# Sparse attention scores: low part of the keys on 64 partitions, multiplied with the high part of the queries alone

## The chip, the cores and the metric

The kernel runs on one core of a Trainium2 chip. The metric is the device time of one execution in microseconds; lower is better. The profile is one execution recorded by the hardware profiler, and its times count from the start of its span.

## What is computed

The reference is a decoder trunk with two layers over 512 tokens of width 1024. Each layer is a half-step feed-forward part, a token mixer, cross-attention into 256 memory tokens, and another feed-forward part. The mixer of layer 0 is causal pooling; that of layer 1 is native sparse attention with 16 query heads in 4 groups, one key head and one value head per group, and a head width of 64. The part that matters here are the scores of its selected-block and sliding-window branches:

```python
q = q.reshape(B, S, G, R, dh).transpose(0, 2, 3, 1, 4) * dh ** -0.5
...
sc = jnp.einsum('bgrqd,bgqkd->bgrqk', qb, ksel)
...
sc = jnp.einsum('bgrqd,bgkd->bgrqk', qb, kwin)
```

With 512 tokens both branches see every earlier token, so the kernel computes both as causal attention over the same range, each with keys and values of its own, and a third branch over 31 compressed blocks per key head.

## The kernel before, in words

Products run on TensorE in fp32r, a rounded form of fp32. To keep the precision the kernel splits an operand into a high part (the rounded value) and a low part (what is left of it): `split` (L413) lets ScalarE (ACT) copy the source into the high part (L415) and VectorE (DVE) subtract that from the source into the low part (L416). A dense product then takes three matmuls, high x high, high x low and low x high (`mm3`, L401, with L403 to L405). The weights are streamed from DRAM by SP and split in the same way, by ACT (L334) and by DVE or GpSimd (POOL) (L374).

Heads are only 64 wide, so a score product fills half of the 128 rows of the array. The kernel before uses the other half for the low part of the queries. `qproj` (L1259) makes, for each query head, one tile `qst` of 128 partitions: the high part in one half, the low part in the other. For even heads the high part is in partitions 0 to 63, for odd heads in 64 to 127. `kproj` (L1246) makes, for each key head, two tiles `kst`, one with the high and one with the low part of the keys of both branches, and it writes each part twice, to partitions 0 to 63 and to 64 to 127, so that both halves of `qst` meet the same keys. `kproj` therefore issues four ACT copies and four DVE subtractions per key head, each of 64 x 512:

```python
for br in range(2):
    src = kf[br * 64:(br + 1) * 64]
    for r0 in (0, 64):
        self.split([a[r0:r0 + 64, br, :] for a in t], src)
```

`mm4` (L407) then needs two matmuls for a score: `qst` with the high keys (L410) and `qst` with the low keys (L411). It contains all four products of the parts.

`softmax` (L1331) calls `mm4` for each of 64 units (4 groups, 4 query heads, 4 blocks of 128 queries). For the first two blocks one call makes both branches, for the last two there is one call per branch. This gives 96 calls, with 256, 512, 384 or 512 columns each. `cmp_scores` (L1289) multiplies the whole `qst` with compressed keys `kcz`, which stand in both halves of the partitions too.

The order of the work is written out by hand. `NSA_START` is a string that says how the steps of the compressed keys' hidden layer (`hidden`, `cmp_k_hidden`, `cmp_k`), of the first key head and of the first query heads follow each other; `cmp_k_hidden` splits a transposed tile into `hidT`. Then the units run in a loop with softmax, transposes into `pT` (L1369), and products with the values (`values`, L1374 to L1382) three units later. The table `FILL` says how many steps of the next key and query heads' projections go between the units, and `CMP` when the compressed branch's steps run (`cmp_transposed`, L1323, writes `pTc`). Within one engine the instructions run in the order in which they were placed when the program was built; across engines they wait on semaphores.

Of the kernel before, what the change touches and what calls it, by code (L numbers as in the profile page):

```python
# [6 lines left out]
F32 = mybir.dt.float32  # L7
# [388 lines left out]
class Kernel:  # L396
# [9 lines left out]

    def mm4(self, ps, a, b, start, stop, **kw):  # L407

        mm = self.nc.tensor.matmul
        mm(ps, a, b[0], start=start, stop=False, **kw)  # L410
        mm(ps, a, b[1], start=False, stop=stop, **kw)  # L411

    def split(self, hl, src):  # L413

# [680 lines left out]
    def nsa(self, gnext):  # L1095
        nc, small, att = self.nc, self.small, self.att
# [149 lines left out]
        def kproj(g):  # L1246
            ps = self.bank("psk")
            yield from self.dense_steps(ps, ("nsa_w_k", g * P), xg)
            kf = self.tmp("kf")
            nc.vector.tensor_mul(kf, ps, self.rbc)  # L1250
            t = [self.b4("kst") for _ in range(2)]
            for br in range(2):
                src = kf[br * 64:(br + 1) * 64]
                for r0 in (0, 64):
                    self.split([a[r0:r0 + 64, br, :] for a in t], src)
            kst[g] = t
            yield

        def qproj(g, cs=(0, 1)):  # L1259
            for c in cs:  # L1260
                ps = self.bank("psq")
                yield from self.dense_steps(ps, (W_NSA, g * 256 + c * P), xg)
                for b in range(2):
                    t = self.b2("qst")
                    self.split((t[b * 64:(b + 1) * 64], t[(1 - b) * 64:(2 - b) * 64]), ps[b * 64:(b + 1) * 64])
                    qst[g, 2 * c + b] = t
                yield

# [9 lines left out]
        def fill(g):  # L1278
            if g < NG - 1:
                yield from kproj(g + 1)  # L1280
                yield from qproj(g + 1)
            else:
                yield from self.mem_k(1, 0)
            if g > 0:
                yield from wo(2 * g - 2, 2 * g, False)
            if g == NG - 1:
                yield from self.mem_k(1, 1)
# [157 lines left out]
        kc2 = blocks(1)  # L1445
        vproj(1, {})
        parts = {"A": hidden(0, kc), "K": kproj(0), "Q": qproj(0, (0,)), "B": hidden(1, kc2), "R": qproj(0, (1,))}
        for c in NSA_START:
            if c in parts:
# [113 lines left out]
```

## Time and profile before

| what | value |
|---|---|
| three executions | 2070.29, 2070.99, 2071.24 us (median 2070.99) |
| the profiled execution's own time | 2072.0 us |
| its span, first to last instruction | 2070.3 us |
| mean granted TensorE clock | 0.996 |
| TensorE (PE) busy | 2051.1 us, 99% of the span |
| VectorE (DVE) busy | 1549.8 us, 75% |
| ScalarE (ACT) busy | 1128.5 us, 55% |
| GpSimd (POOL) busy | 184.4 us, 9% |

PE stands for matmuls and PEld for loads of their weights, which overlap the matmuls. A matmul's record is longer than its step to the next one, because the ends overlap; so the step from start to start tells what a matmul costs in a dense stretch. A shape such as 128*128 128x512 gives the rows and columns of the weights and the rows and columns of what streams past them.

### The profile page before, as it was taken

To read this page: it belongs to the slowest core of one execution; us is meant where nothing else is said; L and a number is where in the kernel's file an instruction comes from. 1 tells how busy PE (TensorE), PEld (TensorE's weight loads), DVE (VectorE), ACT (ScalarE), POOL (GpSimd) and SP (SyncE) were. 2 spreads that over 40 slices of the span, in tenths; PEclk is the share of its full clock that TensorE was granted. 3 is DMA by queue.
4 is the path that set the end of the run, shared out by engine and by line. 5 is a ranking of instruction groups with operands and counts; after the bars stand their busy time and mean duration, and the time that the engine had idled before them with its cause. 6 is when DMAs were issued, how large, how long until landed. Compare 5 with 4: busy or idle time off the path is not lost.

```text
span 2070.3 us, 33527 instructions
## 1 busy us (share of the span) xinstructions
PE 2051.1 (99%) x12373; PEld 1832.8 (89%) x12373; DVE 1549.8 (75%) x2828; ACT 1128.5 (55%) x2275; POOL 184.4 (9%) x261
## 2 busy tenths in 40 slices
PE   9999999999999999999999999999999999999998
PEld 7899998988889999888999988888998888899997
DVE  8777976965877777688777757788976458777774
ACT  6445555554545445554545545787775545454453
POOL 0000000000000000000000023444552100000000
PEclk9999999999999999999999999999999999999999
DMA  5333323532333332334333234311224223423322
GB/s 163 118 107 115 120 67 103 154 101 61 96 124 97 110 108 65 102 92 132 94 106 112 62 94 122 92 32 42 62 62 137 84 72 94 136 94 107 97 67 77
DMA packets 112501, 200.92 MB, mean 97 GB/s; under 512 B 12624, under 2 KB 20176, under 8 KB 112336
## 3 DMA queue, kind: packets, MB, share of 16 engines
q1 hardware_dynamic: 111920, 198.46, 31.2%
q8 instruction: 97, 1.59, 0.3%
q14 instruction: 68, 0.56, 0.1%
q10 hardware_dynamic: 416, 0.32, 0.1%
HBM read 196.63 MB, written 2.10 MB: 96 GB/s over the span
## 4 chain that ended last, share of the span: by engine, by line
PE 95%; DVE 2%; DMA 1%; ACT 1%; issue 0%; SPq 0%; POOL 0%; DVEq 0%; ACTq 0%
PE psr L405 10%; PE psr L403 10%; PE psr L404 10%; PE psy L404 10%; PE psy L403 10%; PE psy L405 10%; PE pso L1381 2%; PE psq L403 2%; PE psq L404 2%; PE psq L405 2%; PE psg L405 1%; PE psg L403 1%; PE psg L404 1%; PE psf L403 1%; PE psf L405 1%; PE psf L404 1%
## 5 line engine op out<-in xcount | busy, mean ns | idle before, releaser
L334 ACT CAST whl<-wraw 128x512 fp32r<-128x512 f32 (+3 forms) x688 | 416.3, 609 | 345.3 <-PE psy L405 99.5
L374 DVE TENSOR_TENSOR whl<-wraw,whl 128x512 fp32r<-128x512 f32 (+1 forms) x634 | 434.7, 688 | 221.2 <-ACT whl L334 206.5
L403 PE MATMUL psr<-rhs,whl 128*128 128x256 f32 x1764 | 500.3, 284 | 2.2 <-ACT whl L334 2.1
L405 PE MATMUL psr<-rhs,whl 128*128 128x256 f32 x1764 | 499.4, 284 | 0.8 <-DVE whl L374 0.8
L404 PE MATMUL psr<-rhs,whl 128*128 128x256 f32 x1764 | 499.8, 283 | 0.0
L403 PEld LDWEIGHTS psr<-rhs,whl 128*128 128x128 f32 x1764 | 338.9, 192 | 6.6 <-ACT whl L334 3.8
L404 PEld LDWEIGHTS psr<-rhs,whl 128*128 128x128 f32 x1764 | 339.0, 192 | 2.8
L405 PEld LDWEIGHTS psr<-rhs,whl 128*128 128x128 f32 x1764 | 338.7, 192 | 1.6 <-DVE whl L374 1.4
L404 PE MATMUL psy<-hT,whl 128*128 128x512 f32 (+1 forms) x710 | 276.3, 389 | 0.0
L403 PE MATMUL psy<-hT,whl 128*128 128x512 f32 (+1 forms) x710 | 275.9, 389 | 0.0
L405 PE MATMUL psy<-hT,whl 128*128 128x512 f32 (+1 forms) x710 | 275.0, 387 | 0.0
L334 ACT CAST whl<-wsum 128x512 fp32r<-128x512 f32 x252 | 156.7, 622 | 196.2 <-PE psy L405 150.5
L374 DVE TENSOR_TENSOR whl<-wsum,whl 128x512 fp32r<-128x512 f32 x252 | 173.3, 689 | 59.1 <-ACT whl L334 57.2
L405 PEld LDWEIGHTS psy<-hT,whl 128*128 128x128 f32 x710 | 133.4, 188 | 27.8
L404 PEld LDWEIGHTS psy<-hT,whl 128*128 128x128 f32 x710 | 133.6, 188 | 25.6 <-DVE hT L416 1.2
L403 PEld LDWEIGHTS psy<-hT,whl 128*128 128x128 f32 x710 | 133.6, 188 | 25.3
L374 POOL TENSOR_TENSOR whl<-wraw,whl 128x512 fp32r<-128x512 f32 (+2 forms) x54 | 68.2, 1265 | 817.8 <-ACT whl L334 803.7
L730 DVE SCALAR_TENSOR_TENSOR x<-psy,x 128x512 f32<-128x512 f32 x120 | 82.6, 688 | 41.5 <-PE psy L405 40.8
L1362 POOL TENSOR_SCALAR pr<-pr,smn,gates 128x128 f32<-128x128 f32 (+3 forms) x128 | 85.8, 683 | 103.9 <-DVE smn L1360 98.3
L1353 ACT ACTIVATE pr<-pr,mxn 128x128 f32<-128x128 f32 (+3 forms) x128 | 71.3, 559 | 14.3 <-DVE mxn L1349 13.1
L403 PE MATMUL psq<-xg,whl 128*128 128x512 f32 x192 | 76.0, 396 | 0.0
L404 PE MATMUL psq<-xg,whl 128*128 128x512 f32 x192 | 75.6, 394 | 0.0
(305 smaller groups left out, 3933.8 us busy)
## 6 DMA issues: line engine op xcount, KB each, us to landing
wraw<-wts SPq DMA_DIRECT2D x708, 256.0 KB, 2.7
wraw<-wts SPq DMA_DIRECT2D x21, 128.0 KB, 2.5
wraw<-wts SPq DMA_DIRECT2D x14, 192.0 KB, 2.6
x<-xT SPq DMA_DIRECT2D x8, 256.0 KB, 5.4
mraw<-memT SPq DMA_DIRECT2D x4, 512.0 KB, 3.0
out<-y SPq DMA_DIRECT2D x7, 256.0 KB, 2.4
wraw<-wts SPq DMA_DIRECT2D x8, 152.0 KB, 2.1
out<-y ACTq DMA_DIRECT2D x1, 256.0 KB, 3.1
```

The costliest lines, as they stand in the source:

```text
L334: nc.scalar.copy(self.hl[q][:, 0, :w], src[:, :w])
L374: eng.tensor_sub(hl[:, 1, :w], src[:, :w], hl[:, 0, :w].bitcast(F32))
L403: mm(ps, a[0], b[0], start=start, stop=False, **kw)
L404: mm(ps, a[0], b[1], start=False, stop=False, **kw)
L405: mm(ps, a[1], b[0], start=False, stop=stop, **kw)
L730: nc.vector.scalar_tensor_tensor(self.x[m], ps, 0.5, self.x[m], op0=ALU.mult, op1=ALU.add)
L1353: nc.scalar.activation(pr[br][:, :nk], pr[br][:, :nk], AF.Exp, bias=mx[:, br:br + 1], scale=-1.0, accum_out=sums[:, br:br + 1])
L1362: nc.gpsimd.tensor_scalar(pr[br][:, :nk], pr[br][:, :nk], sums[:, br:br + 1], gt[:, i, h * 3 + 1 + br:h * 3 + 2 + br], op0=ALU.mult, op1=A ...
L1381: nc.tensor.matmul(ps[:, c0:c0 + 256], v[br][j][:, g, :], pT[br][:, hl, j, :], start=False, stop=br == 1 and j == 2 * i2 + 1 and hl == 1)
```

## The change

The low part of the keys is written to partitions 0 to 63 only, and the queries' high part always stands in partitions 0 to 63, the low part in 64 to 127. The second matmul of `mm4` uses these 64 partitions alone: it multiplies the high part of the queries with the low part of the keys. The product of both low parts is left out. The high keys are still written to both halves.

```diff
     def mm4(self, ps, a, b, start, stop, **kw):
...
         mm = self.nc.tensor.matmul
         mm(ps, a, b[0], start=start, stop=False, **kw)
-        mm(ps, a, b[1], start=False, stop=stop, **kw)
+        mm(ps, a[:64], b[1][:64], start=False, stop=stop, **kw)
...
             for br in range(2):
                 src = kf[br * 64:(br + 1) * 64]
                 for r0 in (0, 64):
-                    self.split([a[r0:r0 + 64, br, :] for a in t], src)
+                    nc.scalar.copy(t[0][r0:r0 + 64, br, :], src)
+                nc.vector.tensor_sub(t[1][:64, br, :], src, t[0][:64, br, :].bitcast(F32))
             kst[g] = t
...
                 for b in range(2):
                     t = self.b2("qst")
-                    self.split((t[b * 64:(b + 1) * 64], t[(1 - b) * 64:(2 - b) * 64]), ps[b * 64:(b + 1) * 64])
+                    self.split((t[:64], t[64:]), ps[b * 64:(b + 1) * 64])
                     qst[g, 2 * c + b] = t
```

## Rows read from the trace of the kernel before

**Rows 1.** The page, engines: busy us, share of the span, instructions.
```profile
PE   2051.1 (99%) x12373; PEld 1832.8 (89%) x12373; DVE 1549.8 (75%) x2828; ACT 1128.5 (55%) x2275; POOL 184.4 (9%) x261
```

**Rows 2.** The page, chain that ended last, by engine.
```profile
PE 95%; DVE 2%; DMA 1%; ACT 1%; issue 0%; SPq 0%; POOL 0%; DVEq 0%; ACTq 0%
```

**Rows 3.** By stretch: us; busy PE, PEld, DVE, ACT, POOL; granted clock, DMA share, GB/s.
```profile
1290.70:1294.30 3.60, 1.12 (x6) 0.53 (x4) 3.48 (x6) 3.43 (x7) 0.22 (x1) 1.00 0.37 112
1294.30:1301.10 6.80, 6.37 (x24) 5.79 (x25) 4.22 (x12) 2.67 (x8) 2.29 (x2) 0.50 0.30 99
...
1299.00:1545.00 246.00, 242.85 (x1526) 215.88 (x1525) 209.95 (x590) 190.30 (x514) 116.73 (x154) 1.00 0.20 59
```

**Rows 4.** What PE waited for, 1290 to 1545 us: total, times, longest.
```profile
PE psk L403 <- ACT hidT L415: 2.2, 1, 2.2
PE psc L1295 <- DVE qst L416: 1.6, 2, 1.3
PE psk L404 <- DVE hidT L416: 0.7, 1, 0.7
PE pso L1381 <- DVE pT L416: 0.6, 1, 0.6
...
PE pso L1377 <- DVE pTc L416: 0.4, 1, 0.4
```

**Rows 5.** Instructions on kst and qst: ns min/median/max, first and last start.
```profile
L415 ACT CAST kst<-kf x16: 615/618/624, 1290.3 to 1444.8; 64x512 fp32r<-64x512 f32 x16
L416 DVE TENSOR_TENSOR kst<-kf,kst x16: 675/690/1157, 1291.4 to 1445.9; 64x512 fp32r<-64x512 f32 x16
...
L416 DVE TENSOR_TENSOR qst<-psq,qst x16: 683/688/694, 1295.2 to 1468.0; 64x512 fp32r<-64x512 f32 x16
```

**Rows 6.** Timelines of DVE and ACT at key head 0: start, us.
```profile
1291.39 2.83 DVE L416 TENSOR_TENSOR kst<-kf,kst 64x512 fp32r<-64x512 f32 x4
1294.26 0.43 DVE L416 TENSOR_TENSOR hidT<-pst,hidT 128x256 fp32r<-128x256 f32 x1
...
1292.86 0.37 ACT L415 CAST hidT<-pst 128x256 fp32r<-128x256 f32 x1
```

**Rows 7.** Timelines of DVE and PE behind key head 1: start, us, [idle before].
```profile
1334.39 0.68 DVE L416 TENSOR_TENSOR pTc<-pst,pTc 128x512 fp32r<-128x512 f32 x1
...
1334.37 0.28 PE L1377 MATMUL pso<-pTc,vz 128*128 128x256 f32 x1
...
1335.12 0.39 PE L1377 MATMUL pso<-pTc,vz 128*128 128x256 f32 x1 [0.36 <-DVE pTc L416]
```

**Rows 8.** Timeline of DVE at key head 3.
```profile
1442.68 1.40 DVE L416 TENSOR_TENSOR kst<-kf,kst 64x512 fp32r<-64x512 f32 x2
...
1444.82 2.20 DVE L416 TENSOR_TENSOR kst<-kf,kst 64x512 fp32r<-64x512 f32 x2
1447.05 0.76 DVE L416 TENSOR_TENSOR pT<-pst,pT 128x256 fp32r<-128x256 f32 x2
```

**Rows 9.** Second score products: ns min/median/max, first and last start, shapes.
```profile
L411 PE MATMUL pss<-kst,qst x96: 278/388/415, 1300.0 to 1543.5; 128*128 128x512 f32 x48, 128*128 128x384 f32 x32, 128*128 128x256 f32 x16
```

**Rows 10.** Timeline of PE, dense products and transposes.
```profile
1369.78 0.82 PE L1369 MATMUL pst<-identf,pr 128*128 128x128 f32 x6
...
1370.61 0.34 PE L411 MATMUL pss<-kst,qst 128*128 128x384 f32 x1
1370.79 0.34 PE L410 MATMUL pss<-kst,qst 128*128 128x384 f32 x1
...
1371.14 0.39 PE L403 MATMUL psk<-xg,whl 128*128 128x512 f32 x1
1371.37 0.40 PE L404 MATMUL psk<-xg,whl 128*128 128x512 f32 x1
...
1372.07 0.60 PE L1326 MATMUL pst<-identf,pc 128*128 128x128 f32 x4
...
1372.74 0.40 PE L405 MATMUL psk<-xg,whl 128*128 128x512 f32 x1
```

## The prediction, made before the changed kernel was run

> **What bounds the kernel now.** I read the engine shares first, then the chain, then a stretch. PE is busy 99% of the span and DVE 75% [rows 1], and 95% of the chain that ended last is PE's [rows 2]: time comes off only where PE stands still or where its own work gets shorter, and whatever is added to PE's work counts in full. The change touches only the sparse attention of layer 1. From 1299 to 1545 us, where the scores are made, PE is busy 242.85 of 246 us [rows 3], so there is hardly a gap in which a dearer product could hide. The list of PE's waits shows what is left of gaps there [rows 4]: 2.2 us on an ACT copy of hidT, 1.6 us on qst, and three waits on DVE (hidT 0.7, pT 0.6, pTc 0.4). The last three are the ones that this change could reach, as the timelines will show.
>
> **Subtractions taken away.** For each of four key heads the kernel makes four ACT copies and four DVE subtractions of kst; 16 subtractions stand in the trace, 0.69 us at the median [rows 5]. The change keeps the copies and drops two subtractions per head, 8 x 0.69 = 5.5 us of DVE work. Most of it lies beside PE work and gives nothing. It counts where PE waits for a DVE instruction queued behind kst:
> - Head 0: four subtractions hold DVE from 1291.39 for 2.83 us, and hidT's subtraction gets in only at 1294.26 [rows 6]. ACT has hidT's copy done at 1292.86 + 0.37 = 1293.23 [rows 6]. With two of them DVE is free by about 1292.9, after the third copy and its subtraction, so hidT is ready at about 1293.23 + 0.43 = 1293.7 instead of 1294.7: the wait of 0.7 goes. What is late next is ACT: its four kst copies stay, hidT's copy stays behind them, and with it the 2.2 us.
> - Head 1: PE resumes at 1335.12, when pTc's subtraction (from 1334.39) is nearly done [rows 7]; kst stood four times ahead of it in the same queue. 1.4 us less there covers this wait of 0.4.
> - Head 3: two kst subtractions run from 1444.82 for 2.20 us (one of the 16 takes 1.16 us [rows 5]), and pT's behind them start at 1447.05 [rows 8]. One or both fall away: the wait of 0.6 goes.
> Together 0.7 + 0.6 + 0.4 = 1.7 us. Bounds: nothing, if ACT's copies or the order of instructions hold these three back anyway, and 1.7 us plus the clock, below.
>
> **Queries turned round.** For odd heads both parts swap halves: same number of instructions, same shapes; only the copy now crosses halves where the subtraction's output did. Crossing is already among the measured ones: kst copies, half of which cross, take 615 to 624 ns, and qst subtractions, of either kind, 683 to 694 [rows 5]. Cost nothing, and nothing leans on cover. The compressed scores multiply the whole qst with keys that stand in both halves, so they do not change. No DMA, no SP or POOL instruction and no wait is added; the score product waits for both parts of q as before.
>
> **The second product on 64 rows.** This is the term that decides. Each of the 96 pairs L410, L411 (the 96 second ones are in [rows 9]) now has a second product of 64 x 128 between products of 128 x 128. Its columns stay. A product's step to the next goes with the columns: 384 take 0.18 us, 512 take 0.23 [rows 10], so I expect nothing from half the height; a gain is excluded as long as that holds, since the first product of each pair uses all rows and can't run beside it. What the trace does not hold is a change of height: every matmul in it is 128*128. So I bound its cost.
> - Lower end, nothing. The nearest change of kind is from a transpose to an fp32r product. Six transposes and a 384-column product take 1370.61 - 1369.78 = 0.83 us, four and a 512-column product 1372.74 - 1372.07 = 0.67 [rows 10]. Less the products' 0.175 and 0.23 this is 0.655 and 0.44, that is 0.11 per transpose both times and no remainder for the change.
> - Upper end for the weights alone. Loads run ahead under the product before. Where one could not, after the wait at 1335.12, the 256-column product reads 0.39 us instead of 0.28 [rows 7], so an uncovered load costs 0.11. There are two changes of height per pair, into the 64 rows and back, since the next product is always a full one: 192 x 0.11 = 21.1 us if neither load runs ahead.
> I take one uncovered load per pair, 96 x 0.11 = 10.6 us. It lies between, and for not taking zero I have this reason: the transpose keeps the 128 rows, while here a load must go into half of the rows that the running product still uses. I can't derive from rows which of the two loads stays covered.
>
> The Trainium skill speaks against this change: TensorEngine Tiling (Array Packing), section Tiling Modes, under Key Properties, says that changing the tiling mode, not just the tile, drains the engine. No row here shows a product of fewer rows, so the trace can't confirm it; the transposes, which change the kind of product but not the height, show no drain. By that rule the sum would be that of the third rival below.
>
> **Sum.** The profiled execution took 2072.0 us (span 2070.3 and 1.7 around it); it lies 1.0 above the median of 2070.99. 2072.0 + 10.6 - 1.7 = 2080.9; on the scale of the median 2079.9 us.
>
> **Rivals.**
> 1. No price for the height. Then only the waits go: 2070.99 - 1.7 = 2069.3 us, or 2071.0 if ACT holds them. For it: the transposes, and loads that run ahead everywhere else. It includes the case that the change does not do what it says, that a 64-row product is laid out like a full one. It decides if the step behind a second product stays at 0.23 us for 512 columns.
> 2. Faster: no price, and the clock stays up. After the waits of 2.2 and 0.7 the granted clock fell to 0.50 from 1294.3 to 1301.1 [rows 3], the 1.2 GHz level; these 6.8 us at half speed cost 3.4. If the engine's earlier return at about 1293.7 prevents that, the time is 2070.99 - 1.7 - 3.4 = 2065.9 us. Against it: the longer idle time, 2.2 us, remains, and PE did only 1.12 us of work in the 3.6 before the fall.
> 3. A full drain at both changes. Products overlap their ends: a 512-column one is recorded for 0.39 us, but the next starts 0.23 after it [rows 10]. If every change lost this 0.16 and the load's 0.11, it would be 192 x 0.27 = 51.8 us, and the time 2070.99 + 51.8 - 1.7 = 2121.1. It decides if the second product's step grows by a quarter of a microsecond on both sides.
>
> **How the numbers follow.** About 0.2% (4.1 us) is what a measurement of this kernel can tell from no change. My forecast, one to two uncovered loads or a part of one, has 0.40; its own range is 2075 to 2091 (one load per pair 2079.9, two 2090.4). Rival 1 has 0.33, rival 2 0.13, rival 3 0.10. I leave 0.04 for instructions falling into another order: in the trace two kst subtractions of head 3 stand apart from their group [rows 8], though the code issues the four together, so the order is made by a scheduler, and an edit may move it. Of these 0.04 half goes to faster, half to slower. Slower: 0.40 + 0.10 + 0.02 = 0.52; same 0.33; faster 0.15. The range takes in rivals 1 and 2 and both loads uncovered: 2065.5 to 2092, which leaves out the drain and a little beside it.
>
> **What would show it.** Right: the second product of a pair appears as 64*128, its own step or that of the product behind it is 0.11 us longer (0.34 instead of 0.23 for 512 columns), PE's busy time between 1299 and 1545 grows with the stretch by some 10 us, and PE's waits on DVE for hidT, pT and pTc are gone while the 2.2 us on ACT stays. Wrong: steps of 0.23 and 0.18 on either side of a 64-row product (rival 1); a stretch after 1294 us with a clock of 1.00 (rival 2); a step of some 0.5 us (rival 3). If the steps are unchanged and the time still moves by over 4 us without the clock, my view of what is queued behind kst is wrong.

## The result, and the profile after

The changed kernel takes 2100.22 us (median of 4 runs, 2099.9 to 2101.48), the kernel before 2070.88 beside it: a ratio of 1.0145, with a 95% interval of 1.0133 to 1.0157. It is 29.3 us slower. The prediction had said slower, but 2079.9 us and at most 2092.

First the engines and the chain on the page of the changed kernel (columns as in [rows 1] and [rows 2]):

```profile
PE 2083.3 (99%) x12373; PEld 1832.2 (87%) x12373; DVE 1548.0 (74%) x2820; ACT 1128.6 (54%) x2275; POOL 184.3 (9%) x261
...
PE 97%; DVE 1%; DMA 1%; ACT 1%; issue 0%; SPq 0%; POOL 0%; DVEq 0%; ACTq 0%; POOLq 0%
```

PE has as many matmuls as before and reads 32 us more busy time; its weight loads read none more. DVE has lost the eight subtractions. So the time went into PE's products, and a look at the second score products tells which ones (instructions on the score tiles: ns min/median/max, first and last start, shapes):

```profile
L411 PE MATMUL pss<-kst,qst x96: 279/442/502, 1294.7 to 1570.8; 128*128 128x512 f32 x48, 128*128 128x384 f32 x32, 128*128 128x256 f32 x16
L412 PE MATMUL pss<-kst,qst x96: 379/467/502, 1294.9 to 1571.3; 64*128 64x512 f32 x48, 64*128 64x384 f32 x32, 64*128 64x256 f32 x16
```

The new line 412 is the old 411. Its products are 64*128 now, their median is 467 ns instead of 388, and they run from 1294.9 to 1571.3 us, 276.4 us, where those of [rows 9] ran from 1300.0 to 1543.5, 243.5 us. The stretch of the scores became 32.9 us longer. It starts 5.1 us earlier, and what lies behind it keeps its length to within 0.3 us (the span grew by 28.1).

Where in the stretch the time lies shows in the steps between products. The timelines of PE and of its weight loads, at one pair of branches after a transpose (four score products of 384 columns and one dense product of 512):

```profile
1329.28 0.42 PE L411 MATMUL pss<-kst,qst 128*128 128x384 f32 x1
1329.63 0.44 PE L412 MATMUL pss<-kst,qst 64*128 64x384 f32 x1
1330.00 0.44 PE L411 MATMUL pss<-kst,qst 128*128 128x384 f32 x1
1330.37 0.44 PE L412 MATMUL pss<-kst,qst 64*128 64x384 f32 x1
1330.74 0.50 PE L403 MATMUL psq<-xg,whl 128*128 128x512 f32 x1
1331.07 0.40 PE L404 MATMUL psq<-xg,whl 128*128 128x512 f32 x1
...
1329.62 0.18 PEld L412 LDWEIGHTS pss<-kst,qst 64*128 64x128 f32 x1 [0.18 <-issue]
1330.00 0.19 PEld L411 LDWEIGHTS pss<-kst,qst 128*128 128x128 f32 x1 [0.19 <-issue]
1330.36 0.18 PEld L412 LDWEIGHTS pss<-kst,qst 64*128 64x128 f32 x1 [0.18 <-issue]
1330.74 0.19 PEld L403 LDWEIGHTS psq<-xg,whl 128*128 128x128 f32 x1 [0.19 <-issue]
1330.84 0.19 PEld L404 LDWEIGHTS psq<-xg,whl 128*128 128x128 f32 x1
```

A step of 384 columns between two changes of height is 0.37 us, where [rows 10] had 0.18. The loads tell why. Each one across a change of height starts when the product before it is nearly through: L411 is recorded from 1329.28 to 1329.70, and the 64-row weights come at 1329.62. Only the last load, between two full products, runs ahead again: 0.10 us behind L403's own.

Of PE's waits on DVE, the three that the change was to save, 1.7 us, did go (waits of PE between 1290 and 1575 us, to be read against [rows 4]):

```profile
PE psk L403 <- ACT hidT L416: 2.0, 1, 2.0
PE psc L1297 <- DVE qst L417: 1.3, 1, 1.3
```

The granted clock also differs. In the profile after it stays up (a stretch of [rows 3], and the stretch from 82 to 92 us, which lies before anything that was changed; columns as in [rows 3]):

```profile
82.00:92.00 10.00, 9.17 (x62) 8.24 (x61) 8.91 (x16) 6.63 (x14) 0.00 (x0) 1.00 0.70 219
...
1294.30:1301.10 6.80, 6.80 (x43) 5.63 (x42) 3.89 (x12) 5.50 (x14) 3.83 (x5) 1.00 0.51 157
```

The kernel before read 0.50 in the second of these [rows 3] and 0.83 in the first (1.00 is the 2.4 GHz level, 0.50 the 1.2 GHz level, a figure between them a stretch with both):

```profile
82.00:92.00 10.00, 8.27 (x52) 7.78 (x52) 7.06 (x13) 5.56 (x11) 0.00 (x0) 0.83 0.53 178
```

This makes 0.17 x 10 + 0.50 x 6.8 = 5.1 us. That is the earlier start of the scores in this profile, to within the 0.7 us wait that went as well; 1.9 us of it are there already at 1290 us, ahead of the wait on hidT. How little it has to do with the change, the experiments show.

### The profile page after: what moved, and what is told of

Read it like the earlier page. It is cut to its first block, busy times and chain, and to the rows that moved or that the text cites. A ratio compares the mean times of both kernels' runs of the same rounds, so it can differ in the third digit from the quotient of the medians.

```text
span 2098.4 us, 33515 instructions
## 1 busy us (share of the span) xinstructions
PE 2083.3 (99%) x12373; PEld 1832.2 (87%) x12373; DVE 1548.0 (74%) x2820; ACT 1128.6 (54%) x2275; POOL 184.3 (9%) x261
## 4 chain that ended last, share of the span: by engine, by line
PE 97%; DVE 1%; DMA 1%; ACT 1%; issue 0%; SPq 0%; POOL 0%; DVEq 0%; ACTq 0%; POOLq 0%
PE psr L405 10%; PE psr L403 10%; PE psr L404 10%; PE psy L403 10%; PE psy L404 10%; PE psy L405 10%; PE pso L1383 2%; PE psq L403 2%; PE psq L405 2%; PE psq L404 2%; PE pss L412 2%; PE pst L1371 2%; PE psg L405 1%; PE psg L403 1%; PE psg L404 1%; PE psf L403 1%
## 5 line engine op out<-in xcount | busy, mean ns | idle before, releaser
L403 PE MATMUL psr<-rhs,whl 128*128 128x256 f32 x1764 | 499.6, 283 | 1.1 <-ACT whl L334 1.0
L403 PEld LDWEIGHTS psr<-rhs,whl 128*128 128x128 f32 x1764 | 338.0, 192 | 5.2 <-ACT whl L334 2.3
L403 PE MATMUL psy<-hT,whl 128*128 128x512 f32 (+1 forms) x710 | 275.9, 389 | 0.0
L403 PEld LDWEIGHTS psy<-hT,whl 128*128 128x128 f32 x710 | 133.6, 188 | 25.5
L374 POOL TENSOR_TENSOR whl<-wraw,whl 128x512 fp32r<-128x512 f32 (+2 forms) x54 | 69.2, 1284 | 836.4 <-ACT whl L334 829.1
L403 PE MATMUL psq<-xg,whl 128*128 128x512 f32 x192 | 77.7, 404 | 0.0
```

What stands on the lines that cost most here:

```text
L374: eng.tensor_sub(hl[:, 1, :w], src[:, :w], hl[:, 0, :w].bitcast(F32))
L403: mm(ps, a[0], b[0], start=start, stop=False, **kw)
```

## The experiments

Theory A: every change of the array's height, from 128 rows to 64 or back, empties PE before the next weights go in, and costs 0.196 us. This figure came from the steps of the profile after against those before: the three steps around a pair with 512 columns that stands alone grew by 96, 193 and 104 ns, together 0.39 us for two changes. 192 changes make 37.7 us, 9.6 more than the span grew by. Its rivals: the order of instructions or the layout (B), any product with fewer rows (C), the 64-row product by itself (E), and a price by the rows filled (F). Rivals D and G concern the subtractions and the copies.

**full_rows: the same, without the half height.** Two edits on the changed kernel:

```diff
-        mm(ps, a[:64], b[1][:64], start=False, stop=stop, **kw)
+        mm(ps, a, b[1], start=False, stop=stop, **kw)
...
             t = [self.b4("kst") for _ in range(2)]
+            nc.gpsimd.memset(t[1][64:].bitcast(F32), 0.0)
```

> The changed kernel, but with the second product on all 128 rows again; the upper half of the low keys is set to zero by POOL, so the same three products are summed. Theory A (a change of the array's height costs 0.196 us, 192 times = 37.7 us, and all else of the change gained 9.6 us of span): 2100.2 - 37.7 = 2062.5 us, up to 2069 if a part of the 9.6 was the clock by chance. Rival B (the price is the moved order of instructions or the keys' new layout, not the height): it stays above 2090.

Measured: 2068.12 us, ratio to before 0.9988 (0.9979 to 0.9997). The slowdown is gone with the height, though layout, subtractions and turned queries are those of the changed kernel; rival B falls. The 2062.5 us of theory A are missed by 5.6; only its upper end of 2069, kept for the clock, covers the time. The same five products after a transpose (PE's timeline):

```profile
1394.78 0.42 PE L411 MATMUL pss<-kst,qst 128*128 128x384 f32 x1
1395.03 0.34 PE L412 MATMUL pss<-kst,qst 128*128 128x384 f32 x1
1395.21 0.34 PE L411 MATMUL pss<-kst,qst 128*128 128x384 f32 x1
1395.39 0.34 PE L412 MATMUL pss<-kst,qst 128*128 128x384 f32 x1
1395.57 0.39 PE L403 MATMUL psq<-xg,whl 128*128 128x512 f32 x1
1395.80 0.40 PE L404 MATMUL psq<-xg,whl 128*128 128x512 f32 x1
```

From the first start to the last it is 1.02 us, in the changed kernel 1331.07 - 1329.28 = 1.79. Four changes of height: 0.77 / 4 = 0.19 us each. It is spread over the five steps: the one ahead of the first change grew by 0.10 (from 0.25 to 0.35), the three between two changes by 0.19 each, the one behind the last by 0.10 (from 0.23 to 0.33).

**adjacent: the same products, fewer changes.** On the changed kernel:

```diff
-            for br in range(2):
-                if i >= 2:
-                    self.mm4(ps[br][:, :nk], q, [t[:, br, :nk] for t in kst[g]], True, True)
+            if i >= 2:
+                for br in range(2):
+                    nc.tensor.matmul(ps[br][:, :nk], q, kst[g][0][:, br, :nk], start=True, stop=False)
+                for br in range(2):
+                    nc.tensor.matmul(ps[br][:, :nk], q[:64], kst[g][1][:64, br, :nk], start=False, stop=True)
+            for br in range(2):
```

> The changed kernel with the four products of the later query blocks in the order full, full, half, half instead of full, half, full, half: still 96 products of 64 rows, but 128 changes of height instead of 192. Theory A: 64 x 0.196 = 12.5 us less, 2087.7 us, and the step between two 64-row products is 0.23 us for 512 columns. Rival E (each 64-row product is dear by itself, about 0.39 us, wherever it stands): 2100 us.

Measured: 2089.13 us (ratio 1.0088, 1.0074 to 1.0101), so rival E falls. The timeline of PE and of its loads:

```profile
1371.48 0.59 PE L1350 MATMUL pss<-kst,qst 128*128 128x384 f32 x2
1372.01 0.61 PE L1352 MATMUL pss<-kst,qst 64*128 64x384 f32 x2
1372.55 0.50 PE L403 MATMUL psk<-xg,whl 128*128 128x512 f32 x1
1372.89 0.40 PE L404 MATMUL psk<-xg,whl 128*128 128x512 f32 x1
...
1372.01 0.29 PEld L1352 LDWEIGHTS pss<-kst,qst 64*128 64x128 f32 x2 [0.25 <-issue]
1372.55 0.19 PEld L403 LDWEIGHTS psk<-xg,whl 128*128 128x128 f32 x1 [0.25 <-issue]
```

The same five products take 1372.89 - 1371.48 = 1.41 us with two changes: 0.39 over full_rows, 0.195 each. So 0, 2 and 4 changes give 1.02, 1.41 and 1.79. Two 64-row loads following each other take 0.29 us together, one 0.18: between equal heights the second runs ahead as ever. I had expected the step between the two 64-row products at 0.23 for 512 columns; it is 0.34 at the median of 15, because a part of a change's price lies in the step after it. So only sums over a whole group can be compared. The count of 128 changes was wrong by two: the code issues full, full, half, half for every later block, but in the trace the products of one unit stand apart (full and half at 1360.19 us, full and half again at 1362.93), which makes 130.

**rows96: fewer rows, but no change of height?** As full_rows, with the second product on `a[:96]` and `b[1][:96]` and partitions 64 to 95 of the low keys zeroed.

> As full_rows, but the second product takes 96 rows, the last 32 of them zero on the side of the keys. Theory A, in the form that the array has heights of 32, 64 and 128 and 96 rows run in the full one: within 1 us of full_rows, steps of 0.23 us for 512 columns. Rival C (any product that uses fewer rows than its neighbour pays): as the changed kernel, about 2100 us, with steps of 0.42.

Measured: 2068.78 us (ratio 0.9991, 0.9981 to 1.0001). The second score products:

```profile
L412 PE MATMUL pss<-kst,qst x96: 277/392/415, 1296.1 to 1539.1; 96*128 96x512 f32 x48, 96*128 96x384 f32 x32, 96*128 96x256 f32 x16
```

And its PE timeline at one pair:

```profile
1371.11 0.40 PE L412 MATMUL pss<-kst,qst 96*128 96x512 f32 x1
1371.35 0.40 PE L411 MATMUL pss<-kst,qst 128*128 128x512 f32 x1
1371.58 0.40 PE L412 MATMUL pss<-kst,qst 96*128 96x512 f32 x1
1371.82 0.40 PE L403 MATMUL psk<-xg,whl 128*128 128x512 f32 x1
```

The median is 392 ns, a step 0.23 to 0.24 us, as among full products: 96 rows run like 128 and cost nothing, so rival C falls. Fewer rows alone are not the cause.

**rows32: half as many rows again.** On the changed kernel, the second product on 32 rows; it leaves out 32 of the 64 dimensions of the low key parts:

```diff
-        mm(ps, a[:64], b[1][:64], start=False, stop=stop, **kw)
+        mm(ps, a[:32], b[1][:32], start=False, stop=stop, **kw)
```

> The changed kernel with the second product on 32 rows; it leaves out the other 32 of the 64 dimensions of the low keys. Theory A (a change of height empties the array before the next weights go in, whatever the two heights): steps and time as with 64 rows, 2099 to 2102 us. Rival F (the price goes with the rows that are filled anew): clearly less than 0.196 us per change, under 2095 us.

Measured: 2099.89 us (2 runs), ratio 1.0145 (1.0127 to 1.0164), the changed kernel's. Its second score products:

```profile
L412 PE MATMUL pss<-kst,qst x96: 377/466/500, 1294.1 to 1570.4; 32*128 32x512 f32 x48, 32*128 32x384 f32 x32, 32*128 32x256 f32 x16
```

Median 466 ns against 467, stretch 276.3 us against 276.4: the price doesn't go with the number of rows, and rival F falls.

**rows_alone: the half height without the saved subtractions.** On the changed kernel:

```diff
-                    nc.scalar.copy(t[0][r0:r0 + 64, br, :], src)
-                nc.vector.tensor_sub(t[1][:64, br, :], src, t[0][:64, br, :].bitcast(F32))
+                    self.split([a[r0:r0 + 64, br, :] for a in t], src)
```

> The 64-row product alone: the low keys are written to both halves again, with all 16 subtractions; the second product still reads one half. Theory A: the 37.7 us stay; what two subtractions fewer per key head had saved comes back, 1.7 us by the prediction, so 2101 to 2104 us. Rival D (the subtractions are worth most of the 9.6 us): 2107 to 2110.

Measured: 2103.15 us (2101.53 to 2103.91), ratio 1.0154 (1.0139 to 1.017); 2.9 above the changed kernel by the medians, 1.9 by the ratios (0.0009 x 2071), whose intervals overlap. In both profiles the clock stayed up until the last 10 us, and their spans, 2099.8 and 2098.4, differ by 1.4. PE's waits between 1284 and 1580 us:

```profile
PE psk L403 <- ACT hidT L416: 2.2, 1, 2.2
PE psc L1296 <- DVE qst L417: 1.3, 1, 1.3
PE psk L404 <- DVE hidT L417: 0.7, 1, 0.7
PE pso L1382 <- DVE pT L417: 0.6, 1, 0.6
```

The waits on hidT (0.7) and pT (0.6) are back, to the tenth those of [rows 4]; that on pTc is not. So it was the subtractions that held them, and what they are worth is about the 1.7 us of the sum. Rival D, 7 to 10 us, falls.

This run, full_rows and adjacent also show how far the clock goes with the change. The stretch from 1294.3 to 1301.1 us, in full_rows and then in rows_alone:

```profile
1294.30:1301.10 6.80, 6.80 (x41) 6.21 (x41) 3.54 (x11) 5.32 (x14) 3.48 (x5) 0.84 0.50 154
```

```profile
1294.30:1301.10 6.80, 6.80 (x46) 5.82 (x44) 4.08 (x12) 5.49 (x16) 2.94 (x3) 1.00 0.55 173
```

In rows_alone the 0.7 us wait is there and the clock stays at 1.00. In full_rows the wait is down to 0.2 and the clock falls for a part, to 0.84. The wait doesn't decide over the fall. And in adjacent, where PE runs the same products in the same order as in the changed kernel until 1308 us, with the wait on hidT at 0.2 us, the clock fell:

```profile
1290.70:1294.30 3.60, 3.19 (x14) 2.76 (x15) 2.77 (x6) 2.48 (x6) 0.14 (x1) 0.68 0.44 125
```

**turned: the queries alone.** On the kernel before:

```diff
-                    self.split((t[b * 64:(b + 1) * 64], t[(1 - b) * 64:(2 - b) * 64]), ps[b * 64:(b + 1) * 64])
+                    self.split((t[:64], t[64:]), ps[b * 64:(b + 1) * 64])
```

> The kernel before with the turned queries alone (the high part always in the lower half; low keys in both halves, full products). Every theory: no change, 2070 to 2071 us, within 0.2%. If it is slower by more, crossing halves has a price that I had put at nothing.

Measured: 2069.89 us beside 2070.06, ratio 1.0 (0.9991 to 1.0009). Crossing the halves is free, to within 0.1%.

**pool_copy: ACT's copies shortened too.** What is left behind the subtractions is PE's wait of 2.1 us on ACT. From full_rows, half of the copies of the high key part go to POOL:

```diff
-                for r0 in (0, 64):
-                    nc.scalar.copy(t[0][r0:r0 + 64, br, :], src)
+                nc.scalar.copy(t[0][:64, br, :], src)
+                nc.gpsimd.tensor_copy(t[0][64:, br, :], src)
```

> full_rows with the second copy of the high keys on POOL instead of ACT. PE's longest wait left, 2.1 us for ACT's copy of hidT behind four key copies, loses two of them, 1.25 us; if that also spares the fall of the clock, more. 2064 to 2067 us against 2068.1 of full_rows. Rival G (POOL's copies are slow and arrive late, or crowd DVE): 2068 or more.

Measured: 2068.01 us, ratio 0.9988 (0.9979 to 0.9997), full_rows' own: no gain that shows, as rival G has it. The time alone could not tell 1 us, but PE's waits add up to 4.5 us here and to 4.4 in full_rows. The three longest:

```profile
PE psc L1298 <- DVE qst L417: 1.7, 2, 1.3
PE psk L404 <- DVE hidT L417: 1.2, 1, 1.2
PE psk L403 <- ACT hidT L416: 0.9, 1, 0.9
```

The wait on ACT fell from 2.1 to 0.9 us, and one of 1.2 on DVE's hidT took its place. The timelines of DVE and POOL at key head 0 fit this:

```profile
1289.41 1.94 DVE L1258 TENSOR_TENSOR kst<-kf,kst 64x512 fp32r<-64x512 f32 x2
1291.38 0.42 DVE L417 TENSOR_TENSOR hidT<-pst,hidT 128x256 fp32r<-128x256 f32 x1
...
1288.86 1.95 POOL L1257 CAST kst<-kf 64x512 fp32r<-64x512 f32 x2 [1.28 <-DVE kf L1251]
```

DVE's two subtractions take 1.94 us while POOL copies beside them, and hidT's stands behind them; in the changed kernel the same two, as one row of DVE's timeline there, took 1.39:

```profile
1289.63 1.39 DVE L1257 TENSOR_TENSOR kst<-kf,kst 64x512 fp32r<-64x512 f32 x2
```

That the one slows the other is what the overlap suggests; it was not tried by itself.

## Why the prediction was wrong, point by point

**What bounds the kernel: right.** PE had no gap in the score stretch that a dearer product could hide in. The changed kernel reads 32 us more of busy PE and a span 28.1 longer, with 97% of the chain on PE.

**The failing step: "one uncovered load per pair, 96 x 0.11 = 10.6 us".** It was wrong in the count, and the price left out a part.
- The count. Both changes of a pair cost, 192 and not 96. For 0, 2 and 4 changes the sums of five products rise by 0.39 and then 0.38 us, and the whole time follows: adjacent has 130 changes (31 groups and 34 pairs that stand alone, two each) and lies 21.0 us above full_rows, the changed kernel with 192 of them 32.1.
- The price. A change costs 0.19 us, not 0.11. The 0.11 for an uncovered load stands, and in the steps too: behind the wait of [rows 7] the load starts only with its product at 1335.12, and the next product starts 0.23 us later, where the 256-column product of 1334.37 has a step of 0.12:

```profile
1334.49 0.27 PE L1369 MATMUL pst<-identf,pr 128*128 128x128 f32 x1
...
1335.35 0.52 PE L1381 MATMUL pso<-pT,nv 128*128 128x256 f32 x3
...
1335.12 0.19 PEld L1377 LDWEIGHTS pso<-pTc,vz 128*128 128x128 f32 x1 [0.61 <-DVE pTc L416]
```

What the price left out lies ahead of the load: across a change it doesn't start until the product before it is nearly through. Against full_rows, step by step, a full product ahead of a 64-row one takes 0.093 us more at the median, one behind it, whose own load comes late, 0.104, and the 64-row product, which has both, 0.194.

My reason for a price, that the load goes into rows which the running product still uses, doesn't hold: so does every load of full_rows, and so does the second 64-row load of adjacent, and these run ahead.

The 192 x 0.11 = 21.1 that I gave as an upper end was none, because it held the loads and nothing for running out, and so the range ended at 2092.

**The lower end misled as well.** The transposes cost no change, which is true, but they are 128 rows high as their neighbours are. A row that lacks the property in question bounds nothing. I saw that no product of another height stood in the trace, and then should have given the third rival more than 0.10.

**Rival 3, the drain, is the right mechanism at too high a price.** It put 0.16 of lost overlap and 0.11 of load at each change, 0.27, and 2121.1 us. Measured: 0.19. The load is as it said, but only half of the overlap is lost: the next load begins 0.08 us before the recorded end of the product before it (1329.62 against 1329.70), and 0.27 - 0.08 is 0.19. The Trainium skill's rule (TensorEngine Tiling (Array Packing), Tiling Modes, Key Properties), that a change of the tiling mode drains the engine, agrees with the trace: the price goes with changes of height, not with products (adjacent), and 32 rows pay what 64 do. The page gives no price.

**Rival 1 (no price) and rival 2 (no price, and the clock) fall** for the change itself; full_rows, where the height stays, does what rival 1 said of the rest: 2068.1 against 2069.3. As to the clock, it did stay up in the profile after, but not because of this change: it fell partly in full_rows and adjacent, which have the same subtractions and queries, stayed up in rows_alone, which has the old subtractions, and between 82 and 92 us it differs too, 0.83 to 1.00, where no instruction was changed.

**The subtractions: right in what waits on them.** 1.7 us were forecast; full_rows is 2.3 below the kernel before, and rows_alone 1.9 to 2.9 above the changed one, 1.4 by the two spans in which the clock stayed up alike. The 2.3 us need not be waits alone: the mean granted clock is 0.996 in 19 of the 21 executions of the kernel before that belong to this comparison and 0.997 or 0.998 in 9 of the 11 of full_rows, and a thousandth of the time is 2.1 us. hidT and pT went as described, and the wait of 2 us on ACT stayed as described. pTc's wait stayed away in rows_alone too, so I have not shown that it was kst that held it.

**The turned queries: right,** by the run of that name.

**The sum with the measured term.** By medians, 2100.22 - 2068.12 = 32.1 us for 192 changes, 0.167 each; adjacent has 2089.13 - 2068.12 = 21.0 for 130 of them, 0.162. It is nearly linear in the changes: with adjacent's price and the relief of full_rows, 2070.88 + 192 x 0.162 - 2.3 = 2099.7 us, and 2100.22 were measured.

**Steps against times, and what stays open.** The matmuls of full_rows and of the changed kernel stand in the same order in both traces, so their steps can be compared one by one. The steps at the 192 changes are 36.5 us longer in sum, 0.190 each (adjacent: 24.6 for 130, 0.189); the 0.196 came from a pair with 512 columns, and the 16 pairs with 256 columns make 0.175 in the mean. In the rest of the score stretch full_rows takes 2.8 us more, nearly all of it in 15 steps, among them waits that the changed kernel lacks, and its scores start 1.0 us later, behind a stretch in which its clock fell. 36.5 - 2.8 - 1.0 = 32.7, and the spans differ by 32.8, so the steps and the times agree. What in the engine holds the load back across a change, and when the clock falls, no run here settles.

## What to carry to other kernels

Keep the height of the array the same from one product to the next: between full products, one of 64 or 32 rows costs 0.19 us on each side, 0.09 until the product ahead has run out and 0.10 for a load that can't run ahead, and zeros that fill it up to 128 rows cost a memset per key head beside the path (2068.1 against 2100.2 us). If the short products must stay short, put them next to each other, since only changes count, and see in the trace whether they stayed so. The good part of this change was elsewhere, in subtractions that stood in DVE's queue ahead of what PE waited for, and it could be had without the short product; it is worth some 0.1% (0.9988 in full_rows, of which the clock may be a part).

## What I had not expected of the hardware

- Half the height saves nothing and costs: a 64-row product alone in a row of full ones takes a step of 0.37 us instead of 0.18 at 384 columns, and so does a full one between two of them.
- 96 rows are as good as 128 (median 392 ns, steps 0.23 to 0.24), 32 as dear as 64 (466 against 467 ns).
- A load of fewer rows is hardly shorter (181 ns at 32 rows, 0.18 us at 64, 0.19 at 128).
